# Order of the expert loop: a small expert's three units side by side, and the large weights' splits at three other places

## The chip, the cores and the metric

The kernel runs on one core of a Trainium2 chip. TensorE multiplies matrices and writes its results to PSUM, which has eight banks here called `ps`. ScalarE (ACT) and VectorE (DVE) read PSUM and work on SBUF, GpSimd (POOL) does a little, and SyncE (SP) issues the transfers from HBM. The metric is the device time of one execution in microseconds, as the median of three runs.

## What is computed

Two layers of a decoder trunk over 256 tokens of width 1024. The change lies in the last stage, the routed experts of layer 1:

```
logits = t @ router                       # t: 256 x 1024, 8 experts
top_val, top_idx = top_k(logits, 2)
gates = softmax of the two, 0 elsewhere   # 256 x 8
for e in range(8):
    out += gates[:, e:e+1] * ((silu(t @ w_gate[e]) * (t @ w_up[e])) @ w_down[e])
x = x + out
```

Each expert has D_FF = 2816, so three matrices of 1024 x 2816 numbers in float32. The output must agree with the float32 reference.

## The kernel before

The expert stage does not compute all 256 tokens for all experts. It sorts the experts by their number of tokens. The four with the most tokens are "large" (up to 128 tokens each), the four others are "small" (up to 64, `HALFP`). One-hot matrices gather an expert's tokens (`gather_split`, `gather_all`: matmuls of the tokens with the one-hots) and scatter its results back into the residual (`scatter`).

An expert's weights are cut into FC = 11 chunks of 256 hidden columns, and each chunk into three units of 1 MB: two units for gate and up (`gu`, half of the 1024 input rows each), and one for down. For every chunk the engines do this: TensorE computes gate and up over both units into one bank; ScalarE takes Silu of the one half, and VectorE multiplies it with the other (`ff_act`, `sm_act`); TensorE transposes the product (`ff_tr`: two transposes, `sm_tr`: one) and the result is copied back to SBUF; TensorE multiplies it with the down unit and adds into the two accumulator banks of that expert (`ys`), which stay open over its eleven chunks.

Large and small experts differ in how the products are made.

- Large (`ff_gu`, `ff_dn`, matmuls on lines 517 to 519): each weight unit is split into a rounded part `wh` (a ScalarE copy of 128x2048) and a rest `wl` (a VectorE subtraction), and every product is three matmuls of 128x512 in the rounded format. One unit is 12 matmuls. The split frees the buffer that the unit was loaded into.
- Small (`sm_gu`, `sm_dn`): the weights go into TensorE as float32, unsplit, in products with 64 columns of the stationary operand, two side by side. The trace records 16 matmuls for a gate/up unit and 8 for a down unit. The buffer is free when TensorE has used it.

`Stream` holds the units' buffers: five called `raw`, and others borrowed from tiles that are done (`xres`, `xg`, `more`, `fl`). Units are loaded in the order in which they are used (`srcs`). A large unit is split by `ahead(most)`, which makes one split if fewer than `most` (here HL = 4, the number of `wh`/`wl` buffers) are ready. Every engine works its instructions in the order in which this code issues them, and SyncE does so with the loads.

The loop runs over `items`: large chunk 0, 1, 2, 3 alone, then a large and a small chunk by turns, the small ones LAG = 4 chunks behind, then the last small chunks alone. For each item it issues the first gate/up unit, the transposes of the item before, a split, the second gate/up unit, the activation, and the down product of the item before. So in a pair of items (a cycle, below) TensorE does: large unit, small transpose, large unit, small down product, small unit, large transposes, small unit, large down product. An expert's scatter follows one item after its last chunk. While the first large expert runs, the tokens of the small experts and of the next large ones are gathered at the ends of some cycles (two gathers each; four cycles for the second and third large expert, four for the last), with one-hots made just ahead of the first of them.

Of the kernel before, what the change touches and what calls it, by code (L numbers as in the profile page):

```python
# [19 lines left out]
P = 128  # L20
EPS = 1e-6
NEG = -1e30
FC = 11
# [26 lines left out]
HL = 4  # L50
# [3 lines left out]
BIG = 4  # L54
HALFP = 64
LAG = 4
# [338 lines left out]
def kernel(ctx: ExitStack, tc: tile.TileContext, a, out: bass.AP):  # L395
# [32 lines left out]
    def pa():  # L428
        return rec.tile(psp, [P, 512], F32, "ps", 8, name="ps")
# [337 lines left out]
    def ff_gu(st, xs, gu, u, ahead=True):  # L767
        wh, wl = st.next(ahead)
        for b in range(len(xs)):
            for kk in range(4):  # L770
                k = 4 * u + kk
                mm3(gu[b], xs[b][0][:, k, :], xs[b][1][:, k, :], wh[:, kk * 512:(kk + 1) * 512],
                    wl[:, kk * 512:(kk + 1) * 512], k == 0, k == 7)

    def ff_act(gu, scales=None, act=None):
        hs = []
        for b in range(len(gu)):
            si = tw(256)
            hh = tw(256)
            if scales:  # L780
                tact(si, gu[b][:, 0:256], AF.Silu, scale=scales[b])
                V.scalar_tensor_tensor(hh, gu[b][:, 256:512], scales[b], si, op0=OP.mult, op1=OP.mult)
            else:
                (act or tact)(si, gu[b][:, 0:256], AF.Silu)
                V.tensor_tensor(hh, gu[b][:, 256:512], si, OP.mult)
            hs.append(hh)
        return hs

    def ff_tr(hs):
        n = 2 * len(hs) * P  # L790
# [79 lines left out]
    for g in range(2):  # L870
        ps = [pa() for i in range(2)]
        for u in range(2):
            wh, wl = split(raw0[u]) if g == 0 else unit(a["w0"][2 + u])
            for kk in range(4):
                k = 4 * u + kk
# [8 lines left out]
        for c in range(4):  # L884
            j = 4 * g + c
# [93 lines left out]
    for b in range(2):  # L979
        y = tw()  # L980
# [555 lines left out]
    def large_split(src):  # L1536
        x = large_tile()
        S.activation(x[0], src, AF.Copy)
        V.tensor_tensor(x[1], src, x[0].bitcast(F32), OP.subtract)
        return x  # L1540


    def sm_gu(xs, gu, u):
        w = st.next(False)
        for kk in range(4):
            k = 4 * u + kk
            wv = w[:, kk * 512:(kk + 1) * 512].rearrange("p (g f) -> p g f", g=2)
            for i in range(2):
                mmx(gu[i * HALFP:(i + 1) * HALFP, 0:256].rearrange("p (g f) -> p g f", g=2), xs[:, k],
                    wv[:, :, i * P:(i + 1) * P], k == 0, k == 7)  # L1550
        st.done()

    def sm_act(gu):
        si, hh = tw(P), tw(P)
        tact(si, gu[:, 0:P], AF.Silu)
        V.tensor_tensor(hh, gu[:, P:256], si, OP.mult)
        return hh

    def sm_tr(hh):
# [19 lines left out]
        return lambda: gtile([P, 2048], F32, n, 2) if n == "xres" else mo([P, 2048], n)  # L1579


    items = []
    for g in range(BIG * FC + LAG):
        if g < BIG * FC:
            items.append((False, *divmod(g, FC)))
        if g >= LAG:
            items.append((True, *divmod(g - LAG, FC)))
    regs = {}

    def source(r, j):  # L1590

        if r == 0:
            return a["moe"][j]

        def at_run():
            if r not in regs:
                regs[r] = nc.values_load(ids[0:1, r:r + 1], engines=[mybir.EngineType.SP], min_val=0, max_val=7)
            return a["moe"][bass.ds(regs[r] * (3 * FC) + j, 1)].rearrange("u p c -> p (u c)")
        return at_run

    srcs, whole = [], []
    for i in range(len(items) + 1):
        for it, js in ((items[i] if i < len(items) else None, (0, 1)), (items[i - 1] if i else None, (2,))):
            for j in js if it else ():
                srcs.append(source(it[1] + (BIG if it[0] else 0), 3 * it[2] + j))
                whole.append(it[0])
# [12 lines left out]
    ys, ohs, ohts, hs, pend = {}, {}, {}, {}, None  # L1619
    N = len(items)  # L1620
    for i in range(N + 1):
        it = items[i] if i < N else None
        was = items[i - 1] if i else None
        alone = not (it and was and it[0] != was[0])
        if it:
            sm, p, c = it
            gu = pa()
            xsp = xs[:, p] if sm else [xb]
            sm_gu(xsp, gu, 0) if sm else ff_gu(st, xsp, [gu], 0, False)
        if was:  # L1630
            t = sm_tr(hs[was]) if was[0] else ff_tr(hs[was])
        st.ahead(HL if alone or it[0] else HL - 1)
        if it:
            sm_gu(xsp, gu, 1) if sm else ff_gu(st, xsp, [gu], 1, False)
            hs[it] = sm_act(gu) if sm else ff_act([gu])
            if not sm and c == FC - 1 and p < BIG - 1:
                xb = large_split(xl[:, p % 2])
        if alone or it[0]:
            st.ahead(HL)
        if was:  # L1640
            wsm, wp, wc = was
            if wc == 0:
                ys[wsm] = [pa(), pa()]
            (sm_dn if wsm else lambda t, y, *f: ff_dn(st, t, [y], *f, False))(t, ys[wsm], wc == 0, wc == FC - 1)
            if alone:
                st.ahead(HL)
        if pend:
            scatter(*pend)
            pend = None
        if was and was[2] == FC - 1:  # L1650
            r = was[1] + (BIG if was[0] else 0)
            pend = (ohts[was[0]], y_split(ys[was[0]]), lambda b, r=r: gateo[:, b, r:r + 1], x3, i == N)
        if not it:
            continue
        if c == 0:
            ohs[sm] = both_halves(BIG + p) if sm else one_hots(p, 1)[:, :, 0]
        if c == 1:
            ohts[sm] = oht_of(ohs[sm][:, 0], ohs[sm][:, 1])
        if sm:
            continue  # L1660
        if p == 0 and c < LAG:
            for k in range(2 * c, 2 * c + 2):
                gather_all(k, oh_s, xs)
        if p == 0 and LAG + 2 <= c < LAG + 6:
            if c == LAG + 2:
                xl, oh_l = mo([P, 2, 8, P], "xg0"), one_hots(1, 2)
            for k in range(2 * (c - LAG - 2), 2 * (c - LAG - 1)):
                gather_all(k, oh_l, xl)
        if p == 1 and 2 <= c < 6:
            if c == 2:  # L1670
                oh_l = one_hots(3, 1)
            for k in range(2 * c - 4, 2 * c - 2):
                gather_all(k, oh_l, xl[:, 0:1])
    scatter(*pend)
    man.close()


# [177 lines left out]
```

## Time and profile before

| | |
|---|---|
| Median of three runs | 1151.35 us (1151.13 to 1151.51) |
| The profiled execution | 1150.8 us |
| Its span | 1148.9 us |
| TensorE matmuls busy | 1124.3 us (98% of the span) |
| VectorE busy | 714.2 us (62%) |
| ScalarE busy | 587.3 us (51%) |
| Read from HBM | 345.95 MB |
| Chain that ended last | PE 84%, DMA 7%, DVE 5%, ACT 3% |

The expert loop fills the span from about 477 us on. A busy time of TensorE is modelled from the starts of its matmuls, so a share of 98% does not say that no instruction could be faster; the starts of the blocks tell more. In the timeline, blocks of the same form are one row, with the start of the first matmul and their number. A block's length is read here from its start to the start of the next.

### The profile page before, as it was taken

What the parts mean: (1) busy time and instruction counts of PE and PEld (TensorE: products, weight loads), DVE (VectorE), ACT (ScalarE), POOL (GpSimd) and SP (SyncE); (2) the same over time, 40 slices, a digit from 0 to 9 for tenths busy, and PEclk for the clock granted to TensorE, in tenths of its full rate; (3) what the DMA queues carried; (4) which work ended last, traced back from release to release, by engine and by line L of the source; (5) the groups of instructions that cost most, each with busy time, mean ns of one, the idle gap of its engine ahead of it and who ended that gap; (6) DMA issues with size and microseconds to landing.
All of it is one profiled execution on the core that took longest, in us unless ns stands there. A gap on an engine that the chain in (4) does not pass through costs nothing.

```text
span 1148.9 us, 16368 instructions
## 1 busy us (share of the span) xinstructions
PE 1124.3 (98%) x6100; PEld 825.4 (72%) x6100; DVE 714.2 (62%) x1172; ACT 587.3 (51%) x979; POOL 29.6 (3%) x59
## 2 busy tenths in 40 slices
PE   8999999999999999999999999999999999999997
PEld 7887888888787877876666666666666666666663
DVE  6999954545388877784456456556556556565531
ACT  6858644444378666573545444444444444444421
POOL 1050000000300000000000000000000000000000
PEclk9999999999999999899999999999999999999999
DMA  9651555546344514389999999999999999999994
GB/s 353 224 198 37 195 208 189 189 179 219 112 167 154 216 63 188 117 325 373 374 404 419 399 400 392 393 424 422 421 421 422 422 423 420 422 421 418 421 421 157
DMA packets 52214, 348.14 MB, mean 303 GB/s; under 512 B 5920, under 2 KB 6048, under 8 KB 11680
## 3 DMA queue, kind: packets, MB, share of 16 engines
q1 hardware_dynamic: 52128, 347.02, 76.1%
q8 instruction: 50, 0.82, 0.3%
q14 instruction: 36, 0.29, 0.1%
HBM read 345.95 MB, written 1.05 MB: 302 GB/s over the span
## 4 chain that ended last, share of the span: by engine, by line
PE 84%; DMA 7%; DVE 5%; ACT 3%; issue 1%; SPq 0%; DVEq 0%; ACTq 0%
PE ps L333 21%; PE ps L517 18%; PE ps L519 18%; PE ps L518 18%; PE ps L328 10%; DMA xres<-in_moe_dram 7%; DVE wl L333 2%; ACT wh L333 2%; DVE wl L328 1%; ACT tw L328 1%; DVE xres L333 0%; DVE tw L328 0%; DMA raw<-in_w_dram 0%; DVE tw L333 0%; DVE more L328 0%
## 5 line engine op out<-in xcount | busy, mean ns | idle before, releaser
L333 DVE TENSOR_TENSOR wl<-raw,wh 128x2048 fp32r<-128x2048 f32 x89 | 204.2, 2294 | 149.5 <-ACT wh L333 148.0
L517 PE MATMUL ps<-wh,fh 128*128 128x512 f32 (+2 forms) x720 | 290.9, 404 | 0.0
L518 PE MATMUL ps<-wl,fh 128*128 128x512 f32 (+2 forms) x720 | 280.6, 390 | 0.0
L333 ACT ACTIVATE tw<-ps 128x128 f32<-128x128 f32 (+2 forms) x202 | 72.7, 362 | 312.1 <-PE ps L333 275.6
L333 ACT ACTIVATE wh<-raw 128x2048 fp32r<-128x2048 f32 x89 | 170.0, 1910 | 62.3 <-PE ps L519 57.7
L517 PEld LDWEIGHTS ps<-wh,fh 128*128 128x128 f32 x720 | 136.4, 189 | 28.1
L518 PEld LDWEIGHTS ps<-wl,fh 128*128 128x128 f32 x720 | 136.4, 189 | 24.1
L333 DVE TENSOR_TENSOR tw<-ps,tw 128x256 f32<-128x256 f32 (+3 forms) x158 | 66.7, 427 | 135.6 <-ACT tw L333 135.5
L519 PE MATMUL ps<-wh,fl 128*128 128x512 f32 (+2 forms) x368 | 142.1, 386 | 0.0
L519 PE MATMUL ps<-wh,fh 128*128 128x512 f32 x352 | 139.0, 395 | 0.0
L333 DVE TENSOR_TENSOR wl<-xres,wh 128x2048 fp32r<-128x2048 f32 x39 | 89.3, 2289 | 53.5 <-ACT wh L333 53.5
L333 PE MATMUL ps<-raw,xs 128*64 128x256 f32 x960 | 116.3, 384 | 0.0
L517 PE MATMUL ps<-wh,tw 128*128 128x512 f32 (+1 forms) x276 | 113.9, 413 | 0.7 <-ACT tw L328 0.7
L519 PE MATMUL ps<-wh,tw 128*128 128x512 f32 (+1 forms) x276 | 109.0, 395 | 0.0
L518 PE MATMUL ps<-wl,tw 128*128 128x512 f32 (+1 forms) x276 | 108.8, 394 | 0.0
L333 ACT ACTIVATE wh<-xres 128x2048 fp32r<-128x2048 f32 x39 | 74.8, 1917 | 63.4 <-DMA xres<-in_moe_dram 58.6
L328 DVE TENSOR_TENSOR wl<-raw,wh 128x512 fp32r<-128x512 f32 (+1 forms) x149 | 98.3, 683 | 2.7 <-ACT wh L328 2.7
L333 PEld LDWEIGHTS ps<-raw,xs 128*64 128x64 f32 x960 | 64.8, 137 | 41.3 <-issue 14.5
L328 ACT ACTIVATE wh<-raw 128x512 fp32r<-128x512 f32 (+1 forms) x131 | 74.8, 626 | 20.1 <-PE ps L519 8.6
L519 PEld LDWEIGHTS ps<-wh,fl 128*128 128x128 f32 x368 | 69.1, 188 | 14.3 <-DVE fl L328 0.2
L519 PEld LDWEIGHTS ps<-wh,fh 128*128 128x128 f32 x352 | 66.7, 189 | 14.5
L517 PEld LDWEIGHTS ps<-wh,tw 128*128 128x128 f32 x276 | 52.0, 188 | 26.4 <-issue 15.4
(283 smaller groups left out, 1324.9 us busy)
## 6 DMA issues: line engine op xcount, KB each, us to landing
raw<-in_moe_dram SPq DMA_DIRECT2D x142, 1024.0 KB, 9.6
xres<-in_moe_dram SPq DMA_DIRECT2D x41, 1024.0 KB, 10.5
raw<-in_ffn_dram SPq DMA_DIRECT2D x30, 1024.0 KB, 4.8
xg<-in_moe_dram SPq DMA_DIRECT2D x27, 1024.0 KB, 9.8
more<-in_moe_dram SPq DMA_DIRECT2D x26, 1024.0 KB, 10.8
fl<-in_moe_dram SPq DMA_DIRECT2D x25, 1024.0 KB, 9.7
raw<-in_w_dram SPq DMA_DIRECT2D x23, 1024.0 KB, 5.0
raw<-in_ffn_dram SPq DMA_DIRECT2D x12, 256.0 KB, 3.7
```

The costliest lines, as they stand in the source:

```text
L328: return (self.name, self.cost(fn, args, kw), lambda: real(*args, **kw))
L333: return getattr(self.eng, fn)(*args, **kw)
L517: nc.tensor.matmul(ps, xh, wh, start=start, stop=False)
L518: nc.tensor.matmul(ps, xh, wl, start=False, stop=False)
L519: nc.tensor.matmul(ps, xl, wh, start=False, stop=stop)
```

## The change

The loop over items is replaced by a list of steps that is written out once per cycle (`steps`). A step is a kind (`gu0`, `gu1`, `tr`, `dn`, `late` for a scatter, `more` for a split, `rest` for gathers and one-hot transposes) and a chunk. In a cycle with a large chunk `l`, the large one before `l0`, a small chunk `s` and the small one before `s0`, the order is: transposes of `l0`, first unit of `l`, any scatter, transpose of `s0`, down product of `l0`, second unit of `l`, gathers, down product of `s0`, both units of `s`. Splits are issued behind each `tr` and behind each large `dn`. The loads follow the new order of use (`used`).

```diff
-    items = []
-    for g in range(BIG * FC + LAG):
-        if g < BIG * FC:
-            items.append((False, *divmod(g, FC)))
-        if g >= LAG:
-            items.append((True, *divmod(g - LAG, FC)))
+    steps = []
+    for g in range(BIG * FC + LAG + 1):
+        l, l0, s, s0 = chunk(False, g), chunk(False, g - 1), chunk(True, g - LAG), chunk(True, g - LAG - 1)
+        if l and s0:
+            o = [("tr", l0), ("gu0", l), ("late", None), ("tr", s0), ("dn", l0), ("gu1", l), ("rest", l),
+                 ("dn", s0), ("gu0", s), ("gu1", s)]
+        elif l0:
+            o = [("gu0", l), ("tr", l0), ("gu0", s if not l else None), ("tr", s0), ("gu1", l), ("more", l), ("dn", l0),
+                 ("late" if l else "", None), ("rest", l), ("dn", s0), ("gu0", s if l else None), ("gu1", s)]
+        else:
+            o = [("gu0", l or s), ("tr", s0), ("gu1", l or s), ("more", l), ("dn", s0), ("late", None), ("rest", l)]
+        steps += [(k, it) for k, it in o if it or k == "late"]
...
+    used = [(k, it) for k, it in steps if k in unit_of]
+    srcs = [source(it[1] + (BIG if it[0] else 0), 3 * it[2] + unit_of[k]) for k, it in used]
...
-            sm_gu(xsp, gu, 0) if sm else ff_gu(st, xsp, [gu], 0, False)
-        if was:
-            t = sm_tr(hs[was]) if was[0] else ff_tr(hs[was])
-        st.ahead(HL if alone or it[0] else HL - 1)
...
-        if alone or it[0]:
-            st.ahead(HL)
...
+        elif k == "tr":
+            ts[sm] = sm_tr(hs[sm]) if sm else ff_tr(hs[sm])
+            st.ahead(HL)
+        elif k == "dn":
...
+                ff_dn(st, ts[sm], [ys[sm]], c == 0, c == FC - 1, False)
                 st.ahead(HL)
...
+            if c == FC - 1:
+                r = p + (BIG if sm else 0)
+                pend.append((ohts[sm], y_split(ys[sm]), lambda b, r=r: gateo[:, b, r:r + 1], x3, n == len(steps) - 2))
+        else:
+            for e in list(ohs):
+                if n >= ohs[e][0] + 5:
+                    o = ohs.pop(e)[1]
+                    ohts[e] = oht_of(o[:, 0], o[:, 1])
```

TensorE, the small block of a plain cycle before: `fh` is a large expert's tokens and `xs` a small one's, `cp,tw` is a transpose, and `wh,tw` a large down product.

```order
L519 MATMUL ps<-wh,fh 128x512
L333 MATMUL ps<-raw,tw 64x512 x4
L333 MATMUL ps<-xg_7332,xs 64x256 x8
L333 MATMUL ps<-cp,tw 128x128 x2
L333 MATMUL ps<-raw,xs 64x256 x8
L517 MATMUL ps<-wh,tw 128x512
```

The same place after the change:

```order
L519 MATMUL ps<-wh,fh 128x512
L333 MATMUL ps<-xg_7298,tw 64x512 x4
L333 MATMUL ps<-raw,xs 64x256 x8
L333 MATMUL ps<-xres,xs 64x256 x8
L333 MATMUL ps<-cp,tw 128x128 x2
L517 MATMUL ps<-wh,fh 128x512
```

The two transposes moved from between the small units to behind them, and a large gate/up unit follows them, no longer the large down product.

ScalarE in one plain cycle before: `wh` are the splits' copies, 128x256 from `ps` are the large chunk's Silu and its transposed product, and 128x128 the small chunk's.

```order
L333 ACTIVATE tw_9260<-ps_9225 128x256
L333 ACTIVATE tw_9284<-ps_9281 128x256
L333 ACTIVATE wh_9288<-raw_9167 128x2048
L333 ACTIVATE tw_9304<-ps_9270 128x128
L333 ACTIVATE wh_9308<-xres_9211 128x2048
L333 ACTIVATE tw_9341<-ps_9339 128x128
L333 ACTIVATE wh_9343<-raw_9246 128x2048
```

And after the change:

```order
L333 ACTIVATE tw_9304<-ps_9301 128x256
L333 ACTIVATE wh_9308<-raw_9211 128x2048
L333 ACTIVATE tw_9329<-ps_9327 128x128
L333 ACTIVATE wh_9331<-raw_9234 128x2048
L333 ACTIVATE wh_9349<-raw_9252 128x2048
L333 ACTIVATE tw_9367<-ps_9314 128x256
L333 ACTIVATE tw_9398<-ps_9377 128x128
```

Two copies now stand next to each other behind the small transposed product, and the small Silu (128x128, last row) follows the large one with no copy between; before it stood behind a copy.

TensorE at the first gathers for the large experts, before: `tw,xnh` and `tw,xnl` are the gathers' matmuls, with the one-hots in `tw`.

```order
L519 MATMUL ps<-wh,fh 128x512
L333 MATMUL ps<-xg_5240,tw 64x512 x4
L333 MATMUL ps<-tw,xnh 128x256 x2
L333 MATMUL ps<-tw,xnl 128x256 x2
L333 MATMUL ps<-tw,xnh 128x256 x2
L333 MATMUL ps<-tw,xnl 128x256 x2
L333 MATMUL ps<-raw,xs 64x256 x8
```

After the change:

```order
L519 MATMUL ps<-wh,fh 128x512
L333 MATMUL ps<-tw,xnh 128x256 x2
L333 MATMUL ps<-tw,xnl 128x256 x2
L333 MATMUL ps<-tw,xnh 128x256 x2
L333 MATMUL ps<-tw,xnl 128x256 x2
L333 MATMUL ps<-xg_5252,tw 64x512 x4
L333 MATMUL ps<-raw,xs 64x256 x8
```

The small down product (64x512) moved from ahead of the gathers to behind them.

## Rows read from the trace of the kernel before

**Rows 1.** Stretches: busy time (and instructions) of PE, PEld, DVE, ACT, POOL, granted clock, DMA share, GB/s.

```profile
560.00:740.00 180.00, 179.50 (x994) 120.39 (x993) 99.43 (x93) 86.17 (x100) 0.00 (x0) 1.00 0.99 399
740.00:1100.00 360.00, 359.36 (x1952) 240.51 (x1951) 208.43 (x183) 167.71 (x179) 0.00 (x0) 1.00 1.01 421
1131.00:1132.00 1.00, 1.00 (x12) 0.55 (x8) 0.00 (x0) 0.00 (x0) 0.00 (x0) 1.00 0.00 0
```

**Rows 2.** Waits of TensorE, 480 us to the end: total, times, longest.

```profile
PE ps L333 <- DVE tw L333: 1.9, 4, 0.6
```

**Rows 3.** Timeline of TensorE, one plain cycle: start, length, instruction, number.

```profile
880.42 1.94 PE L333 MATMUL ps<-raw,tw 128*64 128x512 f32 x8
882.19 1.90 PE L333 MATMUL ps<-more,xs 128*64 128x256 f32 x16
884.01 0.44 PE L333 MATMUL ps<-cp,tw 128*128 128x128 f32 x2
884.38 1.95 PE L333 MATMUL ps<-raw,xs 128*64 128x256 f32 x16
886.26 0.50 PE L517 MATMUL ps<-wh,tw 128*128 128x512 f32 x1
...
889.16 0.39 PE L517 MATMUL ps<-wh,fh 128*128 128x512 f32 x1
...
891.92 0.48 PE L517 MATMUL ps<-wh,fh 128*128 128x512 f32 x1
...
894.85 1.94 PE L333 MATMUL ps<-raw,tw 128*64 128x512 f32 x8
```

**Rows 4.** Timeline of TensorE, the last small down product.

```profile
1136.71 1.94 PE L333 MATMUL ps<-xg,tw 128*64 128x512 f32 x8 [0.37 <-ACT tw L333]
```

**Rows 5.** Timeline of TensorE, a small unit followed by a small down product.

```profile
1113.48 1.95 PE L333 MATMUL ps<-fl,xs 128*64 128x256 f32 x16
1115.26 1.89 PE L333 MATMUL ps<-raw,tw 128*64 128x512 f32 x8
```

**Rows 6.** Timeline of TensorE, two transposes between large products.

```profile
874.48 0.38 PE L333 MATMUL ps<-cp,tw 128*128 128x128 f32 x2
874.61 0.48 PE L517 MATMUL ps<-wh,fh 128*128 128x512 f32 x1
...
877.45 0.27 PE L333 MATMUL ps<-cp,tw 128*128 128x128 f32 x1
```

**Rows 7.** Timeline of TensorE, small down products around a cycle with gathers.

```profile
574.10 1.94 PE L333 MATMUL ps<-raw,tw 128*64 128x512 f32 x8
...
589.83 1.51 PE L333 MATMUL ps<-raw,tw 128*64 128x512 f32 x6
```

**Rows 8.** Timeline of TensorE, the first gathers for the large experts.

```profile
541.81 1.94 PE L333 MATMUL ps<-xg,tw 128*64 128x512 f32 x8
544.37 0.63 PE L333 MATMUL ps<-tw,xnh 128*128 128x256 f32 x2 [0.62 <-DVE tw L333]
544.84 0.40 PE L333 MATMUL ps<-tw,xnl 128*128 128x256 f32 x2
545.08 0.40 PE L333 MATMUL ps<-tw,xnh 128*128 128x256 f32 x2
```

**Rows 9.** Timeline of VectorE at the same place: a split's subtraction and the one-hots.

```profile
541.27 2.29 DVE L333 TENSOR_TENSOR wl<-raw,wh 128x2048 fp32r<-128x2048 f32 x1 [2.84 <-ACT wh L333]
...
543.81 0.75 DVE L333 TENSOR_TENSOR tw<-c,poso 128x256 fp32r<-128x256 f32 x2
```

**Rows 10.** Groups by form, 740 to 1100 us: busy, mean ns, idle before, releasers.

```profile
L333 ACT ACTIVATE wh<-xres 128x2048 fp32r<-128x2048 f32 x24 | 46.0, 1917 | 62.5 <-DMA xres<-in_moe_dram 57.8 <-DVE tw L333 4.7
...
L333 DVE SCALAR_TENSOR_TENSOR xres<-ps,gateo,xres 128x512 f32<-128x512 f32 x16 | 10.9, 742 | 0.0
```

**Rows 11.** Timeline of TensorE, small down products around a cycle with a large expert's scatter.

```profile
788.99 1.94 PE L333 MATMUL ps<-fl,tw 128*64 128x512 f32 x8
...
805.62 1.94 PE L333 MATMUL ps<-raw,tw 128*64 128x512 f32 x8
```

More of the change, by code (lines that the diff above doesn't have):

```diff
@@ L1579, in place, with chunk @@
         return lambda: gtile([P, 2048], F32, n, 2) if n == "xres" else mo([P, 2048], n)
[L1582 to L1587 removed]
+    def chunk(sm, g):
+        return (sm, *divmod(g, FC)) if 0 <= g < BIG * FC else None
+    steps = []
[10 more added lines that the diff above has]
+        steps += [(k, it) for k, it in o if it or k == "late"]
     regs = {}
@@ L1599, in source @@
         return at_run
[L1601 to L1606, printed above, removed]
+    unit_of = {"gu0": 0, "gu1": 1, "dn": 2}
+    used = [(k, it) for k, it in steps if k in unit_of]
+    srcs = [source(it[1] + (BIG if it[0] else 0), 3 * it[2] + unit_of[k]) for k, it in used]
+    whole = [it[0] for k, it in used]
     st = Stream(srcs, ([(place("xres"), 999), (place("xg0"), XG)],
@@ L1618 @@
     ov = out.rearrange("(b p) d -> p b d", p=P)
[L1619 to L1628, printed above, removed]
-            sm_gu(xsp, gu, 0) if sm else ff_gu(st, xsp, [gu], 0, False)
-        if was:
-            t = sm_tr(hs[was]) if was[0] else ff_tr(hs[was])
-        st.ahead(HL if alone or it[0] else HL - 1)
[L1633 to L1637, printed above, removed]
-        if alone or it[0]:
-            st.ahead(HL)
[L1640 to L1645, printed above, removed]
-                st.ahead(HL)
[L1647 to L1673, printed above, removed]
@@ L1674 @@
-    scatter(*pend)
+    gu, hs, ts, ys, ohs, ohts, pend = {}, {}, {}, {}, {}, {}, []
+    for n, (k, it) in enumerate(steps):
+        if k == "late":
+            while pend:
+                scatter(*pend.pop(0))
+            continue
+        sm, p, c = it
+        if k == "more":
+            st.ahead(HL)
+        elif k in ("gu0", "gu1"):
+            if k == "gu0":
+                gu[sm] = pa()
+            if sm:
+                sm_gu(xs[:, p], gu[sm], unit_of[k])
+            else:
+                ff_gu(st, [xb], [gu[sm]], unit_of[k], False)
+            if k == "gu1":
+                hs[sm] = sm_act(gu[sm]) if sm else ff_act([gu[sm]])
+                if not sm and c == FC - 1 and p < BIG - 1:
+                    xb = large_split(xl[:, p % 2])
+                if c == 0:
+                    ohs[sm] = n, both_halves(BIG + p) if sm else one_hots(p, 1)[:, :, 0]
+        elif k == "tr":
+            ts[sm] = sm_tr(hs[sm]) if sm else ff_tr(hs[sm])
+            st.ahead(HL)
+        elif k == "dn":
+            if c == 0:
+                ys[sm] = [pa(), pa()]
+            if sm:
+                sm_dn(ts[sm], ys[sm], c == 0, c == FC - 1)
+            else:
+                ff_dn(st, ts[sm], [ys[sm]], c == 0, c == FC - 1, False)
+                st.ahead(HL)
+            if c == FC - 1:
+                r = p + (BIG if sm else 0)
+                pend.append((ohts[sm], y_split(ys[sm]), lambda b, r=r: gateo[:, b, r:r + 1], x3, n == len(steps) - 2))
+        else:
+            for e in list(ohs):
+                if n >= ohs[e][0] + 5:
+                    o = ohs.pop(e)[1]
+                    ohts[e] = oht_of(o[:, 0], o[:, 1])
+            if p == 0 and c < LAG:
+                for j in range(2 * c, 2 * c + 2):
+                    gather_all(j, oh_s, xs)
+            if p == 0 and LAG + 2 <= c < LAG + 6:
+                if c == LAG + 2:
+                    xl, oh_l = mo([P, 2, 8, P], "xg0"), one_hots(1, 2)
+                for j in range(2 * (c - LAG - 2), 2 * (c - LAG - 1)):
+                    gather_all(j, oh_l, xl)
+            if p == 1 and 2 <= c < 6:
+                if c == 2:
+                    oh_l = one_hots(3, 1)
+                for j in range(2 * c - 4, 2 * c - 2):
+                    gather_all(j, oh_l, xl[:, 0:1])
```

## Prediction

> **What bounds the kernel now.** I read the table of stretches first: it shows which stage could be limited by what. From 560 to 740 us TensorE is busy for 179.50 of 180 us while the transfers run at 399 GB/s; from 740 to 1100 us TensorE is again busy almost throughout, and the transfers run flat at 421 GB/s with a share of 1.01 [rows 1]. So two resources look full, and a busy TensorE is only modelled. The table of waits decides between them: from 480 us to the end TensorE's matmuls wait for VectorE 1.9 us in all, four times, and no row names a transfer [rows 2]. Then the timeline of one plain cycle, 880.42 to 894.85 us: TensorE runs one block after another without a hole, and the cycle takes 14.43 us [rows 3]. The expert stage is therefore bound by TensorE's instruction stream, with the transfers just keeping up. The margin of the transfers is seen at the end: nothing moves any more from 1131 us on [rows 1], and the last unit is used at 1136.71 us [rows 4]. Until then 5.7 us can be gained before the last transfer itself is late.
>
> **The plain cycle (39 of them).** The instructions stay the same; their neighbours change. The pieces before, from the starts [rows 3]: small down product 1.77, first small gate/up unit 1.82, two transposes 0.37, second small unit 1.88, large down product 2.90, first large gate/up unit with the single transpose behind it 2.76, second large unit 2.93; the sum is 14.43. After the change the two transposes stand behind both small units and ahead of a large unit. A small unit that is followed by 64-wide products takes 1.78 [rows 5], and the other keeps 1.82. A pair of transposes ahead of a large unit took 0.13, and the large unit behind it 2.84 [rows 6]; but there a large product stood ahead of the pair, not a small one, so the other bound for the pair is the 0.37 of now. The large down product gets the single transpose ahead of it (2.90 + 0.02), and the second large unit loses it: 2.93 less the 0.08 between 2.84 and 2.76, which is 2.85. Sum: 1.77 + 1.78 + 1.82 + 2.84 + 2.92 + 2.85 = 13.98, plus 0.13 to 0.37, which is 14.11 to 14.35. The saving is 0.08 to 0.32 us a cycle. Since the new pair has the neighbour of the one row on its left and of the other on its right I take the middle, 0.2: 39 × 0.2 = 7.8 us (3.1 to 12.5).
>
> The row shows that the 64-wide products and the full-width transposes next to each other cost time at each change between them. [...]
>
> **Gathers in eight cycles.** They now stand between two full-width neighbours on one side: ahead of the small block, behind the large unit. Before, a cycle with them took 15.73 us [rows 7], 1.30 more than the plain one. Four pairs at the 0.24 between 544.84 and 545.08 [rows 8] are 0.96. That is 0.34 saved in each; four of the eight have half the columns, so I count 2.5 us in all.
>
> **The gathers' first cycle, twice: a new wait.** The gathers need the one-hot matrices, which VectorE makes just ahead of them. Before, the small down product lies over most of that: it starts at 541.81, the gathers start at 544.37, and 0.62 of that is waiting [rows 8]. VectorE meanwhile runs a split's subtraction from 541.27 for 2.29 us and makes the one-hots at 543.81 [rows 9]. After the change the gathers come directly behind the large unit, so the down product covers nothing. The third split is issued right behind the large down product, whose end lies 2.85 us ahead of that point; with 1.92 us of copy [rows 10] and 2.29 of subtraction it ends some 1.4 us after it, where before it ended 541.27 + 2.29 − 541.81 = 1.75 after it. So the wait is about the whole 2.56 − 0.05, which is 1.9 more than the 0.62, twice: 3.8 us lost. If VectorE were free, the wait would still be some 1.2 us (1.2 lost in all); if the split had to wait for its transfer as ScalarE now does in the late stretch, 57.8 us in 24 copies or 2.4 us each [rows 10], it would be 8.6. Behind the waiting gathers stand the small products; only TensorE waits for them.
>
> **Scatters of the large experts, three in the loop.** Before, such a cycle takes 16.63 us [rows 11], 2.20 more than the plain one, since the eight full-width products stand among 64-wide ones. Now they follow a large unit: eight at 2.76/12 = 0.23 are 1.84. Saved: 3 × 0.36 = 1.1 us. But a new wait comes with it: the next large down product opens the accumulators of a new expert and needs two of the eight banks, at a point where the small accumulators (two), the open gate/up accumulator, four scatter results and one transpose hold all eight. VectorE empties the scatter results at 10.9/16 = 0.68 us each [rows 10], behind a 2.29 us subtraction. The wait is between nothing and four of these, 2.7; the first of the four ends about when the down product needs its second bank, so I take 0.7 each, 2.1 us in all (0 to 8.1).
>
> **What costs nothing.** The splits are three a cycle as before, about 1.92 us of ScalarE and 2.29 of VectorE each in a cycle of 14 us. ScalarE's Silu of the small expert no longer has a split ahead of it, but its result is needed only behind the next large unit, so nothing is gained there; the large expert's product is ready behind the third subtraction, some 2 us after its unit, and is needed behind the whole small block of 5.4 us. If a third split waited over 3.4 us for its transfer, that cover would be gone. On SyncE the loads keep their number and follow the order of use; the first fourteen units are the same.
>
> **Sum.** −7.8 − 2.5 + 3.8 − 1.1 + 2.1 = −5.5 us. Of the gain some 1.5 us lie before 740 us, where transfers have room (399 against 421 GB/s), so the transfers may end that much earlier, and 5.7 + 1.5 = 7.2 covers it. The profiled execution took 1150.8 us with its launch, 0.55 below the median of 1151.35; 1150.8 − 5.5 = 1145.3, and against the median 1145.8.
>
> **Rivals.**
> *The transfers set the end.* For it: 421 GB/s without a dip for 360 us, and ScalarE already waits 57.8 us for transfers there [rows 1, 10]. A large unit is now split about one cycle ahead of its use, so it must land some 14 us early. Against it: TensorE does not wait for a transfer yet [rows 2]. Then only the early 1.5 us stay: 1149.8. [...] Chance 0.2.
>
> *VectorE's queue becomes the gate: slower.* The place is the five points where TensorE now meets a VectorE result directly (two gathers, three scatters), each behind a subtraction. At the upper bounds they cost 8.6 + 8.1 instead of 5.9, 10.8 us more, and the time is 1156.6; halfway 1151. It decides from the point where the five waits are on average 1.1 us longer than I take them. For it: the two existing waits of this kind are just there [rows 2, 8]. Against it: VectorE is idle for 40% of the late stretch [rows 1]. Chance 0.2, at 1151 to 1157.
>
> *The change of neighbours is worth nothing.* If the pair costs its 0.37 wherever it stands, the term is 3.1 instead of 7.8, and the time 1150.5. Chance 0.12.
>
> **How the numbers follow.** The forecast, 1145.8, has a chance of 0.48, with a range of its own of 1142 to 1149. About 0.2% (2.3 us) is what a measurement of this kernel can tell from no change, so "same" is 1149.05 to 1153.65. Faster: 0.48, a third of the first rival and of the third, 0.59. Slower: the upper half of the second rival and a little for what I have not seen, 0.19. Same: 0.22. The best case, all terms at their good ends, is limited by the transfers: 5.7 us and an early gain of some 6, which is about 1139.5; the range reaches from 1140 to 1153.5 and leaves out the worst case of VectorE.
>
> **What would show it.** Plain cycles of 14.1 to 14.35 us between the small down products; two transposes ahead of a large unit with under 0.37 us; gather cycles at about 1 us above plain, but two of them with a wait for VectorE of 2 to 3 us; a wait of under 1 us at the large down product behind three scatters; the last unit used within a few us of its landing. It is wrong if plain cycles stay at 14.4, if TensorE waits for ScalarE or VectorE in every cycle, or if large units wait for transfers in the last third.

## The result: slower by 1%, and the profile after

The kernel after the change takes 1161.43 us (median of six, 1160.77 to 1163.25) against 1151.24 us before: a ratio of 1.0096 [1.0081, 1.011] (ratios, here and below, are of the means of the runs, with a 95% interval). Slower had the smallest chance in the prediction, and the time lies outside its range.

The span grew by 11.2 us, from 1148.9 to 1160.1. The first view is the table of stretches of the kernel after, with the columns of [rows 1].

```profile
560.00:740.00 180.00, 174.40 (x992) 121.98 (x990) 100.59 (x90) 85.46 (x98) 0.00 (x0) 0.99 0.97 389
740.00:1100.00 360.00, 348.86 (x1904) 241.00 (x1904) 204.65 (x180) 168.72 (x176) 0.00 (x0) 0.99 1.00 411
1145.00:1146.00 1.00, 1.00 (x12) 0.70 (x10) 0.00 (x0) 0.00 (x0) 0.00 (x0) 1.00 0.00 0
```

Before, TensorE was busy in all but 1.1 us of these 540; now 16.7 us are idle. The transfers no longer run flat: 411 GB/s in the long stretch, where it was 421. The dips lie behind the places where TensorE waits, and not in them: through the third of the long cycles below, 960 to 984 us, the transfers move 422 GB/s, and from 984 to 998 us 386. That the stock of loaded units is full again by then, and no buffer free, is how I read it; no run tested it.

The last small down product, of [rows 4], starts at 1148.57 us, 11.9 later; the transfers are done before 1145 us, so they do not set the end.

The plain cycle is what the change was about. TensorE after the change, one cycle from small down product to small down product, which answers to [rows 3, 5, 6]:

```profile
887.14 1.94 PE L333 MATMUL ps<-xg,tw 128*64 128x512 f32 x8
888.91 1.90 PE L333 MATMUL ps<-raw,xs 128*64 128x256 f32 x16
890.64 1.90 PE L333 MATMUL ps<-xres,xs 128*64 128x256 f32 x16
892.46 0.44 PE L333 MATMUL ps<-cp,tw 128*128 128x128 f32 x2
892.66 0.48 PE L517 MATMUL ps<-wh,fh 128*128 128x512 f32 x1
...
895.52 0.48 PE L517 MATMUL ps<-wh,tw 128*128 128x512 f32 x1
...
898.39 0.39 PE L517 MATMUL ps<-wh,fh 128*128 128x512 f32 x1
...
901.24 1.08 PE L333 MATMUL ps<-more,tw 128*64 128x512 f32 x4
```

The cycle takes 14.10 us, 0.34 less than before. So the gain came, and it is larger than forecast. What ate it is in the waits. Waits of TensorE from 480 us to the end (total, times, longest), where [rows 2] had 1.9 us:

```profile
PE ps L333 <- DVE tw L333: 10.9, 11, 2.3
PE ps L517 <- DVE xres L333: 5.6, 3, 1.9
PE ps L517 <- ACT tw L333: 3.0, 3, 1.0
PE ps L333 <- ACT tw L333: 1.3, 2, 0.9
PE ps L519 <- DVE fh L333: 0.4, 2, 0.2
```

The two longest of the first row are the first gathers' (2.35 and 2.21 us, of the size that was forecast); the first of them:

```profile
544.37 0.63 PE L333 MATMUL ps<-tw,xnh 128*128 128x256 f32 x2 [2.35 <-DVE tw L333]
```

The chain that ended last, which before was 84% PE and 7% DMA:

```profile
PE 69%; DMA 18%; DVE 6%; ACT 5%; issue 1%; SPq 0%; DVEq 0%; ACTq 0%
```

Taking the loop cycle by cycle, from one small down product to the next, before and after, gives the account. The three cycles with a large expert's scatter went from 16.63 us each [rows 11] to 20.15, 22.51 and 23.75: +16.5 us. The whole rest of the span went down by 5.3 us. The forecast for the rest was −6.5 (its −5.5 less the +1.0 that it gave the scatters); that the two are so near is luck, since in the rest both the gains and the losses came out larger than forecast. The error that is left lies in three places of the loop. The third, from 960.07 to 983.82 us; first TensorE, then ScalarE and VectorE:

```profile
960.07 1.94 PE L333 MATMUL ps<-more,tw 128*64 128x512 f32 x8
...
966.85 0.44 PE L333 MATMUL ps<-cp,tw 128*128 128x128 f32 x2 [1.39 <-DVE tw L333]
...
969.88 2.01 PE L333 MATMUL ps<-tw 128*128 128x512 f32 x8
971.73 0.27 PE L333 MATMUL ps<-cp,tw 128*128 128x128 f32 x1
973.00 0.50 PE L517 MATMUL ps<-wh,tw 128*128 128x512 f32 x1 [1.00 <-ACT tw L333]
...
975.82 0.80 PE L517 MATMUL ps<-wh,tw 128*128 128x512 f32 x1 [1.87 <-DVE xres L333]
976.41 0.63 PE L518 MATMUL ps<-wl,tw 128*128 128x512 f32 x1
...
983.82 1.94 PE L333 MATMUL ps<-xg,tw 128*64 128x512 f32 x8
```

```profile
970.87 1.91 ACT L333 ACTIVATE wh<-raw 128x2048 fp32r<-128x2048 f32 x1 [3.10 <-DMA raw<-in_moe_dram]
972.68 0.26 ACT L333 ACTIVATE tw<-ps 128x128 f32<-128x128 f32 x1
```

```profile
972.81 2.29 DVE L333 TENSOR_TENSOR wl<-raw,wh 128x2048 fp32r<-128x2048 f32 x1 [4.59 <-ACT wh L333]
975.02 2.72 DVE L333 SCALAR_TENSOR_TENSOR xres<-ps,gateo,xres 128x512 f32<-128x512 f32 x4
```

Read it from ScalarE. The cycle's first split stands in its queue ahead of the copy of the small transposed product. The split waits 3.10 us for its transfer, until 970.87. The copy (128x128) runs behind it at 972.68, although its transpose was issued at 971.73. That copy frees a bank: the large down product, which opens a new expert, waits 1.00 us for it, and 1.87 us more for the second bank, which the first of the scatter's sums on VectorE frees. These sums stand behind the same split's subtraction, and so begin at 975.02. VectorE's rows show that it kept the order of its queue here: the scatter's products were issued from 969.88 on and done by 971.89, VectorE stood idle until 972.81, and yet its sums of them run behind the subtraction. ScalarE's rows do not show the same of ScalarE, since the copy's transpose came at 971.73, when the split already ran.

Then the clock. Stretches of the kernel after, as in [rows 1]; the number before the DMA share is TensorE's granted clock:

```profile
544.90:548.30 3.40, 3.40 (x13) 1.83 (x14) 0.00 (x0) 0.95 (x2) 0.00 (x0) 0.50 1.02 424
657.50:660.90 3.40, 3.40 (x13) 1.78 (x14) 0.00 (x0) 0.73 (x2) 0.00 (x0) 0.51 1.02 424
807.70:811.10 3.40, 3.20 (x8) 2.53 (x9) 3.40 (x5) 0.00 (x0) 0.00 (x0) 0.50 1.02 424
975.00:981.80 6.80, 5.98 (x14) 4.78 (x15) 4.94 (x6) 2.01 (x2) 0.00 (x0) 0.50 1.01 422
```

At such waits, from 0.9 us before their end to 0.5 us behind it, the clock falls to 0.5 for 3.4 or 6.8 us, and the matmuls of 976.41 start 0.43 us apart instead of 0.23. TensorE's 16.0 busy us in these four rows hold 8.0 us of work at full clock, so the lower clock costs 8.0 us beside the waits themselves. Before, the granted clock was 1.00 from 480 to 1130 us. It does not fall at every such wait: the first of the three scatter cycles has waits of 1.02 us (at 632.64) and 1.86 us (at 635.46) in the same places as the third, and its clock stayed up:

```profile
633.00:637.00 4.00, 2.14 (x10) 1.45 (x9) 4.00 (x5) 1.91 (x1) 0.00 (x0) 1.00 1.01 426
```

The whole account is then: TensorE's waits went from 2.3 us ([rows 2] and the 0.37 of [rows 4]) to 21.2, which is 18.9 more, and the clock costs 8.0, together 26.9 us lost; the span grew by only 11.2, so everything else became 15.7 us shorter.

Why do splits wait? ScalarE by form from 740 to 1100 us, after (busy, mean ns, idle before):

```profile
L333 ACT ACTIVATE wh<-raw 128x2048 fp32r<-128x2048 f32 x71 | 136.0, 1916 | 94.3 <-DMA raw<-in_moe_dram 81.7 <-PE ps L519 12.6
```

Where 24 of the copies waited for transfers before [rows 10], now all read `raw` buffers and wait 81.7 us. A large unit is split about a cycle ahead of its matmuls; a small unit is multiplied as it is. I take it that loads in the order of use bring a small unit about a cycle before it is touched, and a large one at the moment of its split; the run with loads by need tests that.

### The profile page after: what moved, and what is told of

Same layout as the page of the kernel before. It is cut to its first block, busy times and chain, and to the rows that moved or that the text cites. A ratio compares the mean times of both kernels' runs of the same rounds, so it can differ in the third digit from the quotient of the medians.

```text
span 1160.1 us, 16299 instructions
## 1 busy us (share of the span) xinstructions
PE 1116.9 (96%) x6100; PEld 835.5 (72%) x6100; DVE 716.8 (62%) x1172; ACT 592.9 (51%) x979; POOL 29.5 (3%) x59
## 4 chain that ended last, share of the span: by engine, by line
PE 69%; DMA 18%; DVE 6%; ACT 5%; issue 1%; SPq 0%; DVEq 0%; ACTq 0%
DMA raw<-in_moe_dram 17%; PE ps L333 15%; PE ps L517 15%; PE ps L519 15%; PE ps L518 15%; PE ps L328 9%; DVE wl L333 4%; ACT wh L333 4%; DMA raw<-in_w_dram 1%; DVE wl L328 1%; ACT tw L328 1%; DVE tw L328 0%; DVE xres L333 0%; DVE tw L333 0%; SPq L443 0%
## 5 line engine op out<-in xcount | busy, mean ns | idle before, releaser
L333 DVE TENSOR_TENSOR wl<-raw,wh 128x2048 fp32r<-128x2048 f32 x150 | 343.6, 2293 | 217.8 <-ACT wh L333 217.3
L333 ACT ACTIVATE wh<-raw 128x2048 fp32r<-128x2048 f32 x150 | 287.0, 1914 | 174.7 <-DMA raw<-in_moe_dram 95.8
L333 ACT ACTIVATE tw<-ps 128x256 fp32r<-128x256 f32 (+3 forms) x202 | 71.8, 361 | 277.4 <-PE ps L333 246.8
L328 ACT ACTIVATE wh<-raw 128x512 fp32r<-128x512 f32 (+1 forms) x131 | 74.8, 626 | 20.6 <-PE ps L519 8.6
L333 PE MATMUL ps<-raw,xs 128*64 128x256 f32 x704 | 83.6, 380 | 0.0
L333 PEld LDWEIGHTS ps<-raw,xs 128*64 128x64 f32 x704 | 50.3, 137 | 34.2 <-issue 11.2
L517 PEld LDWEIGHTS ps<-wh,tw 128*128 128x128 f32 x276 | 52.9, 192 | 25.1 <-DVE xres L333 6.9
L519 PEld LDWEIGHTS ps<-wh,tw 128*128 128x128 f32 x276 | 52.8, 191 | 12.6 <-DVE tw L328 0.4
L518 PEld LDWEIGHTS ps<-wl,tw 128*128 128x128 f32 x276 | 53.1, 192 | 10.1
```

Of the source, the lines that this page charges most:

```text
L328: return (self.name, self.cost(fn, args, kw), lambda: real(*args, **kw))
L333: return getattr(self.eng, fn)(*args, **kw)
L517: nc.tensor.matmul(ps, xh, wh, start=start, stop=False)
L518: nc.tensor.matmul(ps, xh, wl, start=False, stop=False)
L519: nc.tensor.matmul(ps, xl, wh, start=False, stop=stop)
```

## The experiments

My theory from these rows was of late splits: the load order makes splits wait, with the small copy and a subtraction behind them; apart from that the first gathers wait for one-hots [rows 8, 9], and the clock falls at both. The rivals: VectorE's queue with the scatter's sums is the gate by itself, or the transfers set the pace whatever the order of instructions. Letters in a quoted expectation are that text's own. Twelve kernels were run; each ratio is against the kernel before on the same chip.

**Scatters behind the small down product.**

```diff
-            o = [("tr", l0), ("gu0", l), ("late", None), ("tr", s0), ("dn", l0), ("gu1", l), ("rest", l),
-                 ("dn", s0), ("gu0", s), ("gu1", s)]
+            o = [("tr", l0), ("gu0", l), ("tr", s0), ("dn", l0), ("gu1", l), ("rest", l),
+                 ("dn", s0), ("late", None), ("gu0", s), ("gu1", s)]
```

(Further lines let a result wait until it is over five steps old, so that its scatter comes in the cycle after its last chunk.)

> The changed kernel with one thing undone: an expert's scatter stands behind the small down product again, in the cycle after its last chunk, and no longer between the first large unit and the small transpose. Theory A (the wait is made of late transfers: large units are loaded in the order of use, but are split a whole cycle ahead of it, so the first split of a cycle waits for its transfer on ScalarE, and the small transposed copy, the subtraction and the scatter's results queue behind it): the three long cycles of 20.15, 22.51 and 23.75 us become about 16.5, some 16 us less, but splits still wait for transfers, and waits show up at other places: about 1150. Rival B (the place alone: eight banks and VectorE's order): the three long cycles vanish and nothing takes their place: 1161.4 - 17.9 + 2.5 for seven scatters among 64-wide products, about 1146.

1152.14 us, 1.0012 [0.9999, 1.0026]. TensorE no longer waits for `xres`, and the time is 9.3 us below after; ScalarE still waits 74.8 us for `raw` (95.8 in after). The time is nearer to theory A than to rival B, and waits do show at other places: the first of the moved scatters now falls into the cycle of the second first gathers, which rose from 17.90 to 23.88 us. By itself this run can't tell whether the sums were the loss or only stood in the way of a late split.

**One-hots a cycle earlier.**

```diff
+            if (p, c) in ((0, LAG + 1), (1, 1)):
+                oh_l = one_hots(1, 2) if p == 0 else one_hots(3, 1)
...
-                    xl, oh_l = mo([P, 2, 8, P], "xg0"), one_hots(1, 2)
+                    xl = mo([P, 2, 8, P], "xg0")
...
-                if c == 2:
-                    oh_l = one_hots(3, 1)
```

> The changed kernel with one thing changed: the one-hots of the gathers are made one cycle earlier, so that the first gathers need not wait for VectorE. In the changed kernel the two cycles with this wait and the ones behind them took 18.32 + 16.08 and 17.9 + 16.08 us, where a plain gather cycle takes 15.05: 8.2 us more in all, of which the wait itself is 2.5 and 2.4, and the rest stands at the lower granted clock behind it. Theory A and rival B: no fall of the granted clock at 545 and 658 us, and up to 8 us less, about 1153; under A some of it is lost again, since a faster start only brings the late transfers forward: 1155 to 1159.

1155.18 us, 1.0044 [1.0027, 1.0061]. The first gather cycle fell from 18.32 to 15.04 us and the one behind it from 16.08 to 15.06, so the wait and the clock behind it are gone there; the three scatter cycles stay at 20.77, 22.60 and 23.00.

**The two together.**

> The changed kernel with two of the three cures: scatters behind the small down product, one-hots a cycle early; loads in order of use as in the changed kernel. A (three separate losses: ScalarE's split waits for its transfer with the small transposed copy behind it, VectorE's scatter sums in front of a gate, the first gathers): the two cures add up, 1161.4 - 9.3 - 6.3 = about 1146 (1144 to 1148), no stretch of clock at 0.5 at the first gathers, and ScalarE still waits 70 to 95 us for raw<-in_moe_dram. Rival C (one loss that any of the cures takes away): about 1136 to 1140, little more than all three together (1134.0).

1144.74 us, 0.9952 [0.9935, 0.9969]: the two add up, as its A said (its C gave 1136 to 1140), and ScalarE still waits 81.2 us for transfers.

**Loads by need.** The units are loaded in the order in which they are split or multiplied: a large one counts as used 5.5 units (about a cycle) earlier. Further lines let `Stream` find each unit by `use`.

```diff
+    loads = sorted(range(len(used)), key=lambda i: i if used[i][1][0] else i - 5.5)
+    use = [loads.index(i) for i in range(len(used))]
-    srcs = [source(...) for k, it in used]
+    srcs = [source(...) for k, it in (used[i] for i in loads)]
```

> The changed kernel with another order of loads only: large units are fetched a little ahead of the small units of the cycle before, which is the order in which the splits and the small products need them; the order of work on all engines stays. Theory A: the waits of ScalarE's splits for transfers (95.8 us in 62) nearly vanish, the scatter cycles fall from 20 to 24 us to 17 or 18, and the time to about 1148. Rival B: the scatter cycles stay at 20 us and more: within 2 us of 1161.4. Rival C (the transfers' rate is the bound whatever their order): within 3 us of 1161.

1143.38 us, 0.9941 [0.9924, 0.9957]: 18 us less than after, more than I had expected of it. In the third scatter cycle ScalarE and TensorE now read:

```profile
957.52 0.28 ACT L333 ACTIVATE tw<-ps 128x128 f32<-128x128 f32 x1 [2.46 <-PE ps L333]
957.70 1.91 ACT L333 ACTIVATE wh<-raw 128x2048 fp32r<-128x2048 f32 x1
```

```profile
957.22 0.27 PE L333 MATMUL ps<-cp,tw 128*128 128x128 f32 x1
957.85 0.50 PE L517 MATMUL ps<-wh,tw 128*128 128x512 f32 x1 [0.37 <-ACT tw L333]
```

The copy comes straight behind its transpose, the second bank is free in time, and the cycle takes 16.79 us. ScalarE's waits for transfers in the loop fell from 95.8 us to 1.0. The 23.75 of after is 6.96 more: 1.39 + (1.00 − 0.37) + 1.87 of waits, and 5.98/2 = 3.0 from the clock; sum 6.9.

**The same load order in the kernel before (a control).** The loop of before, its `srcs` sorted in the same way.

> The kernel before, its loop untouched, with its loads sorted by when they are split or multiplied. A (the order of the loads is a loss only through what the change queues behind a waiting split): the kernel before waits 2.3 us in all on TensorE in the loop, so 1149 to 1151, no change. Rival B (a better order of loads is worth its 1.5 per cent in any loop, since transfers set the pace): 1133 to 1141.

1149.62 us, 0.9996 [0.9986, 1.0005]. ScalarE's waits for transfers, 58.6 + 1.4 us in the loop before, are gone there too, and it changes nothing. There, a split that waits has nothing behind it that TensorE needs soon. That a better order of loads is a gain in any loop falls.

**The first split behind the small copy; loads and scatters untouched.**

```diff
-            st.ahead(HL)
+            if not (not sm and steps[n + 2][0] == "late"):
+                st.ahead(HL)
+            if sm and steps[n - 1][0] == "late":
+                st.ahead(HL)
         elif k == "dn":
```

> The changed kernel, its loads and its scatters where they are, but the first of a cycle's three splits is issued behind the small transposed copy and no longer ahead of it (two splits stand there together). A (the stall is the small transposed copy behind a split that waits for its transfer): the waits of TensorE on the copy and on the subtraction at L517 go, the scatter cycles fall from 17.9 to 23.8 us to about 16.2 to 18, and the time to 1146 to 1154. Rival B (the transfers themselves are late, wherever the splits stand): 1158 to 1163, the wait appears at another instruction. C (the scatter sums on VectorE in front of the subtraction are the stall): under 3 us of gain, 1158 to 1161.

1158.16 us, 1.0067 [1.005, 1.0084]: outside the 1146 to 1154 of its A, and inside what both B and C gave. So the time alone speaks against A; the trace shows why. At the third scatter:

```profile
973.68 0.27 PE L333 MATMUL ps<-cp,tw 128*128 128x128 f32 x1
973.71 0.48 PE L517 MATMUL ps<-wh,tw 128*128 128x512 f32 x1
```

There is no wait at the down product, and the three cycles take 16.99, 17.68 and 17.63 us: 14.1 us won. But the cycle's three subtractions now stand in a row on VectorE ahead of the one-hots (VectorE, then TensorE):

```profile
538.91 6.70 DVE L333 TENSOR_TENSOR wl<-raw,wh 128x2048 fp32r<-128x2048 f32 x3 [4.13 <-ACT wh L333]
```

```profile
546.42 0.82 PE L333 MATMUL ps<-tw,xnh 128*128 128x256 f32 x2 [4.12 <-DVE tw L333]
```

The two first gather cycles and the ones behind them went from 18.32, 16.08, 17.90 and 16.08 us to 20.31, 17.11, 20.75 and 16.74 (+6.5). Most of the rest went into smaller waits of the transposes for the large product, which stands behind the third split: 6.2 us in all in after, 11.4 here. So A holds for the three cycles, and the edit brought new losses elsewhere; the next run takes the larger of them away.

**That, with the one-hots early.**

> The first split behind both transposed copies, and one-hots a cycle early; loads and scatters as in the changed kernel. In the run with the splits alone the scatter cycles fell (20.15, 22.51, 23.75 us to 16.99, 17.68, 17.63) but the first gathers, now behind three subtractions in a row on VectorE, waited 4.1 us with the clock at 0.5 for 6.8 us (cycles of 20.31 and 20.75, the next 17.11 and 16.74). A: with the one-hots early these four cycles go to about 15 each, 1158.2 - 14 = 1143 to 1146. Rival B (the transfers set the pace anyway): 1150 to 1156.

1142.05 us, 0.9937 [0.9916, 0.9957]; the four cycles take 15.04, 15.06, 14.93 and 14.93. With loads in the old order and 56.4 us of splits waiting, this is 19 us below after, a little better than its A, and 13 below the run with the one-hots alone (1155.18): most of the loss lay in what was queued behind the late transfer. Not all: with loads by need, the same one-hots and the same scatters, the time is 1134.20 (below), another 7.9 us less. Here the transposes still wait up to 1.53 us for the large product behind a late third split.

**Filling the wait.** Eight matmuls of 128x512 into a bank that nobody reads, ahead of the first gathers, in the kernel with loads by need. They are extra work and change no result.

```diff
+            if (p, c) in ((0, LAG + 2), (1, 2)):
+                z = pa()
+                for j in range(8):
+                    mmx(z, xnh[:, 0, 0:P], xnh[:, 0, 0:512], j == 0, j == 7)
```

The first try had `(0, 0)` in place of `(1, 2)`, a cycle in which nothing waits:

> The kernel with loads by need (1143.4), with eight extra matmuls of 128x512 (0.225 us each, 1.8 us) that multiply into a bank nobody reads, ahead of the first of the gathers in the two cycles in which TensorE waits 2.4 and 2.2 us there and the clock then shows 0.5 for 3.4 us. Nothing else changes. A (a wait of this length is what lowers the clock): the waits shrink to under 0.7 us, the two stretches at 0.5 vanish, and although 3.6 us of work is added the time falls by 2.5 to 4 us, to 1139.5 to 1141. B (the lower clock comes from something else there, the gathers' own form for example): the stretches stay, and the time is 1143 to 1147.

1144.26 us, 0.995 [0.9934, 0.9967]. At the one place that was filled, the two cycles took 17.79 and 15.05 us instead of 18.27 and 16.15; the eight at the wrong place added work, and at the place left open a wait of 2.21 us was now followed by 6.7 us at 0.5 (653.0 to 659.7), where without any fillers it was 3.4, so that its two cycles took 18.24 and 17.34 us instead of 17.87 and 16.10. My placing made it unable to decide, so both places were filled next:

> The kernel with loads by need (1143.4) and eight extra matmuls of 128x512 (0.225 us each, 1.8 us, into a bank nobody reads) ahead of the first gathers of both cycles in which TensorE waits there (at about 541 and 650 us). In the run before, one of the two eights stood at the loop's first cycle, where nothing waits. A (the wait is what lowers the clock): both waits under 0.7 us, no stretch at 0.5 between 480 us and the end, the two cycles together 1.5 to 3 us shorter in spite of 3.6 us of added work: 1140 to 1142. B (the lower clock has another cause there): the stretches stay, 1143.5 to 1147.

1140.65 us, 0.9916 [0.9899, 0.9932], 2.7 us below the kernel without the fillers and inside its A; in the traces the four cycles at the two places are 3.2 us shorter. TensorE at the first place, and the loop's granted clock in one row:

```profile
541.86 2.01 PE L333 MATMUL ps<-xnh 128*128 128x512 f32 x8
544.38 0.63 PE L333 MATMUL ps<-tw,xnh 128*128 128x256 f32 x2 [0.51 <-DVE tw L333]
544.84 0.40 PE L333 MATMUL ps<-tw,xnl 128*128 128x256 f32 x2
545.08 0.40 PE L333 MATMUL ps<-tw,xnh 128*128 128x256 f32 x2
```

```profile
480.00:1130.00 650.00, 645.77 (x3623) 448.22 (x3623) 375.87 (x332) 312.14 (x344) 0.00 (x0) 1.00 0.98 404
```

The gathers start 2.5 us behind the large unit's end at 541.86, with the fillers as without them (in after they start at 544.37, from the same end). What changed is only that TensorE works meanwhile: the gathers' pairs take 0.24 us at full clock, where in after they took up to 0.42, and useless work made the kernel faster.

**Two at a time, and all three.** Loads by need with the one-hots, with the scatters, and with both:

> Loads by need, one-hots a cycle early, scatters where the changed kernel has them. A (separate losses): the two waits at the first gathers with the clock behind them go, 8.0 us of excess of the two cycles and 4.1 of the two behind them, less 0: 1143.4 - 7 to 8 = 1135.5 to 1137. Rival C (the scatters' place is what carries the rest): 1139 to 1142.

1134.20 us, 0.9856 [0.984, 0.9872], a little below its A; its C is out.

> Loads by need, scatters behind the small down product, one-hots where the changed kernel has them. A: only the 0.5 to 0.7 us that each of the scatter cycles is longer than its own work, four to six times, 1143.4 - 2 to 4 = 1139.5 to 1141.5 (with the transfers in time a scatter in the old place stalls little). Rival C (the scatters' place is a large loss of its own, as the 9.3 us of its run alone would say): 1134 to 1137.

1142.35 us, 0.993 [0.9914, 0.9947], a little above its A; its C is out.

> All three edits together: scatter behind the small down product, one-hots a cycle early, loads by need. Theory A: no long waits are left and the granted clock stays at its upper level in the loop: 39 cycles of 14.1 us, gathers and scatters at 1 to 2.2 us, the same tail: 1140 to 1144, unless the transfers at 421 GB/s end it first (then about 1145). Rival C: 1150 or more.

1134.01 us, 0.9866 [0.9849, 0.9882], 6 us below its A. With the loads in order, the scatters' new place is worth 1.0 us, which these few runs can't tell from nothing, and nothing on top of the one-hots; alone it was worth 9.3. So VectorE's sums were hardly a loss of their own; moving them was another way round the late split. The one-hots are worth 9.2 us on top of the loads, a little over the 7 to 8 expected. Both of these kernels are 1.3 to 1.5% faster than before, and 2.3% than after. What bounds the one with two cures (stretches, then TensorE's last small down product):

```profile
560.00:740.00 180.00, 179.63 (x1027) 126.84 (x1024) 105.69 (x93) 90.09 (x101) 0.00 (x0) 1.00 1.01 421
740.00:1100.00 360.00, 357.68 (x1999) 245.22 (x1997) 207.97 (x184) 169.12 (x181) 0.00 (x0) 1.00 1.01 422
1121.00:1122.00 1.00, 0.84 (x4) 0.34 (x6) 0.00 (x0) 0.10 (x1) 0.00 (x0) 1.00 0.00 0
```

```profile
1121.15 1.94 PE L333 MATMUL ps<-fl,tw 128*64 128x512 f32 x8 [0.37 <-ACT tw L333]
```

The transfers run at 421 to 422 GB/s from 560 us on and are done by 1121, when the last small unit is used. So here the transfers end less than 2 us ahead of their last use, which is the prediction's first rival. The last three cycles of the loop show it too: they take 14.72, 14.87 and 15.10 us, about the 14.9 that six units of 1024 KB take at 421 GB/s, and in them TensorE waits 0.4 us three times for a transfer itself, which it never did in the loop before. It would also explain why the third cure adds nothing (1134.01 against 1134.20). That a still shorter cycle would only wait for its units is what I expect; no run tried it.

## Why the prediction was wrong, point by point

The gains came; the losses were mis-sized. The three gains in the sum were put at 11.4 us, and all that is neither a wait nor the lower clock became 15.7 us shorter. The two losses were put at 5.9, and 26.9 came: 18.9 of waits, and 8.0 of the lower clock, which the sum does not have at all.

- *What bounds the kernel now.* Right, with an omission. Six units of 1024 KB at 421 GB/s take 14.9 us, longer than the 14.43 of a cycle [rows 1, 3]: the transfers did not "just keep up", the loop lived on a stock of loaded units. A shorter cycle uses that stock up sooner, so splits meet their transfers; that this is why they meet them, and not the new order alone, no run separates.
- *The plain cycle.* Right mechanism, undersized: 0.34 a cycle and not 0.2, so 12.9 us over the 38 cycles of the loop. The pair of transposes costs 0.20 (892.46 to 892.66), near the low bound of 0.13, and the first small unit is shorter than taken (1.73 for 1.78); the second is as taken (1.82). The third rival (neighbours worth nothing) is out; the pair's low bound, with its 12.5 us, was the better guide.
- *Gathers in eight cycles.* Saved 0.67 in a plain gather cycle (15.73 [rows 7] to 15.06), of which 0.34 is the plain saving; the forecast of 0.34 on top was right. The sum of 2.5 does not follow from its own working, which gives 2.0 (four at 0.34, four at half); but the four with half the columns saved as much as the others (15.63 to 14.93), so 2.7 came.
- *The gathers' first cycle.* The wait was forecast at 2.5 us and measured at 2.35 and 2.21. (Its working let the subtraction end 1.4 us into the wait, and then did not use that figure; in after it ends 1.7 us behind 541.86, much as before.) Not forecast: the clock falls there. The two cycles and their successors lost these waits and some 3.4 us to the clock; loads by need with early one-hots won 9.2 in all there.
- *Scatters.* The term that failed in size. The mechanism was named rightly for one of the two banks, which VectorE's sums free behind a subtraction; it was put at 0.7 us each with 2.7 as the upper bound. The other bank hung on ScalarE's small copy. The two cost 2.9 us each (1.00 + 1.87 in the third), just above that bound; in front of them came a wait for the large product (0.51, 1.46 and 1.39 us), and around two of them the lower clock, 4.6 us. The three cycles' waits are 11.9 us in place of 2.1, and the cycles are 16.5 us longer in place of 1.0.
- *What costs nothing.* The step that failed first: of the 21.2 us of waits, the 14.8 for the large product and at the large down product come from it, and with loads by need 1.1 of them are left. "The splits are three a cycle as before", and the loads "follow the order of use": I counted their time and not their places in the queues. I named one condition, a third split so late that the large product behind it is not ready, and then counted it at nothing; it came about in eight cycles, where the transposes wait 6.2 us in all for that product. What I did not see is what stands behind the first split when it waits (3.10 us in the third scatter cycle): the small transposed copy on ScalarE and, on VectorE, the scatter's sums.
- *Rivals.* The second (VectorE's queue becomes the gate) came nearest: at its five points lie 13.1 of the 21.2 us of waits and all four stretches at the lower clock. Its full price of 1156.6 had the late transfer at the gathers, where none came, lacked it at the scatters, where it came, and lacked the clock. The first (transfers set the end) is wrong for after, whose transfers are done some 6 us before their last use as in the kernel before, and right for the mended kernel, but at 1134 and not at its 1149.8. Neither the best case (1139.5) nor the reason given for it held: 1134.0 was reached, because with loads by need and early one-hots the transfers run at 421 GB/s from 560 us on, where they ran at 399 before [rows 1].

Open: what decides whether a wait lowers the clock, and for how long. In after, waits of 1.00 and 1.87 us with three matmuls between them came with a fall in the third scatter cycle, and 1.02 and 1.86 with none in the first; in the kernel with the splits moved and early one-hots, waits of 1.41 and 1.53 us were followed by matmuls 0.23 us apart, so by no fall; and a wait of 2.21 us was followed by 3.4 us at 0.5 in one kernel and by 6.7 in another. No run varied the length of a wait by itself.

## What to carry to other kernels

When instructions move between engines' queues, ask of each one that can wait for a transfer what stands behind it there, and who waits for that: the control (loads by need, old loop, no gain) shows a late transfer that is free, and the moved split shows one that cost 14 us in three cycles by what stood behind it. Load in the order in which buffers are first touched, not in the order of the matmuls, if some are prepared ahead. A wait on TensorE can bring the slower clock with it (8.0 us beside 21.2 us of waits here), and a few useless matmuls can be cheaper than that (3.6 us of them took 2.7 us off the time).

## What the runs showed of the hardware that was not expected

Waits of 2.35 and 2.2 us in an otherwise full stream were followed by 3.4 us at a granted clock of 0.5; in the kernel with the splits moved a wait of 4.12 us, and in the first run with fillers one of 2.21 us, by 6.7 to 6.8 us. The length of the wait did not settle it: 1.86 us, behind one of 1.02, once left the clock at 1.00 and 1.87, behind one of 1.00, did not. And 3.6 us of extra matmuls in the waits took 2.7 us off the time, with the granted clock at 1.00 from 480 to 1130 us.
